# Four low weight parts of the second attention ordered behind the third-last step of the down chain, and a fourth PSUM bank for the transposes of the output projection

## The chip, the core and the metric

The kernel runs on one NeuronCore of a Trainium2 chip. A core has five engines with a queue each: TensorE (PE; its weight loads are shown apart as PEld), VectorE (DVE), ScalarE (ACT), GpSimd (POOL) and SyncE (SP). Each works its queue in order, and they wait for one another by semaphores. Transfers between HBM and the on-chip SBUF are ordered by SP, POOL and ACT and run on 16 DMA engines. TensorE writes to PSUM, which has eight banks of 128 x 512 fp32 values.

The metric is the device time of one execution in microseconds (us), median of three runs; less is better.

## What is computed

One step of an encoder of two layers in fp32: 1024 prompt tokens (eight tiles of 128) and eight running streams of 16 tokens each (a ninth tile, the "sample" tile, called ST). Cut to what matters:

```
for layer in range(2):
    x = rmsnorm(h, g_attn[layer])
    if layer == 0:  q, k, v = split(x @ w_qkv_a)         # window of 128, ALiBi, sinks
    else:           k, v = split(rmsnorm(h, g_kv) @ w_kv); q = x @ w_q_b   # 8 chunks back, learned bias
    h = h + attend(rmsnorm(q), rmsnorm(k), v) @ w_o[layer]
    h = h + square(relu(rmsnorm(h, g_mlp[layer]) @ w_up[layer])) @ w_down[layer]
```

Model width 1024, 16 heads of 64, 4 key/value heads, 4096 hidden values. The outputs are both token sets after layer 1 and the new keys and values.

## The kernel before, in words

**Numbers in two parts.** Every operand x of a product is cut into a high part (a rounded copy) and a low part (x minus the high part). A product is then three matmuls: high x high, high x low, low x high. `split` (line 125) does it, the high part mostly on ACT (line 128), the low part on DVE (line 134). The attention's projection weights are also multiplied by the norm's gain: `split_g` (line 180) makes the high part of one 128 x 512 slice on POOL (line 185; on ACT in some loads of layer 0) and the low part on DVE (line 190).

**Stages.** Per layer (`run`, line 1318): `attention`, `wo_phase` (the rest of the output projection, norm, and transposes for the MLP), `mlp_up`, `mlp_down`. The two MLP products use a fast matrix multiplication scheme of 20 products a half: `mlp_up` forms seven sums of inputs and weights, writes its results as 20 "forms" to DRAM (`hd`), and `mlp_down` reads them back. The profile has layer 0's down stage up to about 1144 us, then layer 1's attention to about 1618, its output projection to about 1670, and its MLP.

**Order of the work.** A planner (line 1864) simulates the program and orders each engine's instructions by readiness and priority. Some orders are forced by hand: `behind(a, b)` (line 747) puts b after a on their engine, without a wait.

**The down chain** (`mlp_down`, line 965) is 40 products n, each of 36 matmuls into three banks of `ps_c`. For product n DVE makes the low part of the form (`a`, line 134), the low part of the weights (`w`, line 134) and, where the weights are a sum of two slices, that sum in advance (line 1060: `s<-r,r`, or `r<-r,r` in place for the last products). Partial results are added by DVE (line 1174), or copied by ACT (line 1162) and added in DRAM by an accumulating transfer that POOL orders (lines 1165, 1179; line 1092 for whole tiles). `chain` (line 1112) ties all these DVE steps into one fixed order, product by product: low part of form n+1, low part of weights n+1, the sum for n+2, the additions of n. At the end of layer 0 the list of steps reads: ..., low form 38, low weights 38, sum 39, low form 39, low weights 39. The third from its end is therefore the sum for the last product, which starts at 1124.63 us in the profile. The loads of the forms (line 1024) are chained on SP; each takes one of three buffers and goes out when the product three before has left it.

**The start of the second attention** (line 1651). It is emitted after the down stage, with a priority raised by 1000 up to line 1691, so that it is planned into the end of the down chain. `load_block` (line 141) loads the key/value weights in four pieces of two 128-row slices: SP orders the transfer into a "raw" buffer (line 146), POOL makes the high parts, DVE the low ones, eight of each. There are only two raw buffers (line 1322), used in turn; then the first two token tiles X(0), X(1) (line 1421, loads at 1422) take the same two buffers. A buffer is free when both low parts of its piece are made. N(t) transposes X(t) on PE (line 210), cuts it (`hh` on ACT, `hl` on DVE), and K1(t) (lines 217 to 219) multiplies it by the key/value weights.

**The output projection** (`wo_phase`, line 643). `M(t)` finishes tile t in a bank of pool `m` (four banks) and norms it; `S(i)` forms four sums of two tiles on POOL (lines 697 to 700) in single buffers; `T(i)` and the sample tile call `turn` (line 687) 30 times. A turn is four transposes on PE into one bank of pool `g` (three banks), a high part on ACT (`sx`, line 128) and a low part on DVE (`sx`, line 134), after which the bank is free. DVE also makes weight parts for `mlp_up` and norms (line 641) in this time, and the planner puts the first products of `mlp_up` (lines 743 to 745, `ps_x`, `ps_z`) between the turns. `mlp_up` itself uses all eight banks, as does the attention; in `wo_phase` one is unused, the bank in which the attention keeps its projections (`ps_mm`).

Of the kernel before, what the change touches and what calls it, by code (L numbers as in the profile page):

```python
# [94 lines left out]
class Build:  # L95
# [84 lines left out]
    def split_g(self, hi, lo, raw, g, k0, act):  # L180
        nc = self.nc
        for k in range(raw.shape[1]):
            s = self.gcol[:, g * KC + k0 + k : g * KC + k0 + k + 1]
            if "g" in self.engs and not act:
                nc.gpsimd.tensor_scalar(hi[:, k], raw[:, k], s, 1.0, ALU.mult, ALU.mult)
            else:
                z = nc.scalar.activation(hi[:, k], raw[:, k], AF.Copy, scale=s)
                if act:
                    self.behind(self.lp, z)
            nc.vector.scalar_tensor_tensor(  # L190
                lo[:, k], raw[:, k], s, hi[:, k].bitcast(F32), ALU.mult, ALU.subtract
            )

    def wslot(self, kc=KC, n=512):
        self.nw += 1
# [447 lines left out]
    def wo_phase(self, layer, sx, x8, wo):  # L643
        nc = self.nc
        with ExitStack() as st:
            self.psum_pools(st, f"wo{layer}", dict(m=(4, 1), g=(3, 1)), dict(m="m", n="g"))
            work = self.pool(st, f"wow{layer}")
            small = self.pool(st, f"wosm{layer}", 2)
            osp, xs = {}, {}
            lo, hi = slice(0, 512), slice(512, 1024)  # L650

            def O(t, z):
                if t in self.kept:
                    xs[t] = self.kept[t]
                    return
                if len(xs) % 5 < 2:
                    xs[t] = self.rawp.tile([P, D], F32, tag="raw", name="x")
                else:
                    xs[t] = work.tile([P, D], F32, tag="x", name="x", bufs=3)
                nc.sync.dma_start(xs[t], self.xd[t])  # L660
                if t in self.wo_done:
                    return
                with self.tc.high_priority(WO_PRIO) if len(osp) < 2 else nullcontext():
                    load_o(t, z)

            def load_o(t, z):
                o = work.tile([P, 4, P], F32, tag=f"o{z}", name="o")
                oh = work.tile([P, 4, P], F32R, tag=f"oh{z}", name="oh")
                ol = work.tile([P, 4, P], F32R, tag=f"ol{z}", name="ol")
                self.last = oh.bitcast(F32)  # L670
                self.load_halves(layer, 1, t, o, lambda: self.last, nc.vector)
                self.split(oh, ol, o)
                osp[t] = oh, ol

            def M(t):
                x = xs[t]
                for n in range(2) if t not in self.wo_done else ():
                    nn = slice(n * 512, n * 512 + 512)
                    ps = self.psum("m", [P, 512], "ps_wo")
                    self.wo_proj(ps, *osp[t], wo, nn)  # L680
                    nc.vector.tensor_tensor(x[:, nn], ps, x[:, nn], ALU.add)
                if t not in self.wo_done:
                    nc.scalar.dma_start(self.xd[t], x)
                if t not in self.kept:
                    self.norm(small, work.tile([P, D], mybir.dt.bfloat16, tag="junk", name="junk"), x)

            def turn(src, dst, c, d):
                ps = self.psum("n", [P, 4, P], "ps_n")
                for k in range(4):
                    nc.tensor.transpose(ps[:, k, :], src[:, k * P : (k + 1) * P], self.ident)  # L690
                self.split(dst[0][:, d, c], dst[1][:, d, c], ps)

            def S(i):
                x1, x2 = xs[i], xs[i + NT // 2]
                s = self.sums() if i else self.sums0
                tt = nc.gpsimd.tensor_tensor
                tt(s[0], x2[:, lo], x2[:, hi], ALU.add)
                tt(s[1], s[0], x1[:, lo], ALU.subtract)
                tt(s[2], x1[:, lo], x2[:, lo], ALU.subtract)
                tt(s[3], x1[:, hi], s[1], ALU.subtract)  # L700
                return [x1[:, lo], x1[:, hi], x2[:, hi], *s]

            def T(i, src):
                c = slice(i * P, i * P + P)
                for p in (0, 1, 2, 3, 4, 5, 6):
                    turn(src[p], sx[p], c, slice(0, 4))

            order = WO_ORDER[layer]
            ready, pend = set(), []
            z = 0  # L710
            for t in order[:2]:
                O(t, z % 2)
                z += t not in self.wo_done
            for n, t in enumerate(order):
                if n + 2 < NTILE:
                    O(order[n + 2], z % 2)
                    z += order[n + 2] not in self.wo_done
                M(t)
                ready.add(t)
                for f in pend:  # L720
                    f()
                pend = []
                if t == ST:
                    def sample():
                        for h in range(2):
                            turn(xs[ST][:, h * 512 : h * 512 + 512], x8, slice(0, P), slice(4 * h, 4 * h + 4))
                    pend.append(sample)
                elif (t + 4) % NT in ready:
                    i = t % 4
                    T(i, S(i))  # L730
            for f in pend:
                f()
# [232 lines left out]
    def mlp_down(self, layer, out):  # L965
# [3 lines left out]
        with ExitStack() as st:  # L969
# [137 lines left out]
            split_h(0)  # L1107
            split_w(0)
            add_w(1)
            self.dve = None  # L1110

            def chain(z):
                if self.dve is not None:
                    self.behind(self.dve, z)
                self.dve = z
                return z

            self.behind(self.marks[-1], low[0][1])
# [139 lines left out]
    def run(self):  # L1258
# [9 lines left out]
        with ExitStack() as top:  # L1268
# [46 lines left out]
            ]  # L1315
            self.kv_out[1][ST] = flat(nkb_s), flat(nvb_s)
            y = lambda t: y_pf[t * P : (t + 1) * P, :] if t < NT else y_sf
            for layer in range(2):
                with ExitStack() as st:
                    low = st.enter_context(ExitStack())  # L1320
                    pools = (f"raw{layer}", 2), (f"wa{layer}", 1)
                    got = {n: self.pool(low, n, b) for n, b in pools[:: 1 if layer else -1]}
                    self.rawp, self.wa = got[f"raw{layer}"], [got[f"wa{layer}"]]
                    self.nw = 0
                    keep = self.pool(low, f"keep{layer}")
                    self.gb = keep.tile([P, D], F32, tag="gb", name="gb")
                    self.sums = lambda: [
                        keep.tile([P, 512], F32, tag=f"s{n}", name="s") for n in range(4)
                    ]
                    self.sums0 = self.sums()  # L1330
                    self.kept = {}
                    with ExitStack() as more:
                        self.wa.append(self.pool(more, f"wb{layer}"))
                        wo = self.attention(layer)
                    sx, x8, rp = self.up_pools(st, layer)
                    raw0 = self.up_raw(layer, rp, 0)
                    self.wo_phase(layer, sx, x8, wo)
                    low.close()
                    self.mlp_up(layer, sx, x8, rp, raw0)
                self.mlp_down(layer, y if layer else lambda t: self.xd[t])  # L1340
# [24 lines left out]
    def attention(self, layer):  # L1365
# [18 lines left out]
        with ExitStack() as st:  # L1384
# [248 lines left out]
            if A:  # L1633
                X(0)
                self.load_block(wkv, wkv_src, kv0, gkv, [0])
                X(1)
                N(0)
                self.load_block(wkv, wkv_src, kv0, gkv, [2])
                X(ST)
                N(1, "pt")  # L1640
                self.load_block(wkv, wkv_src, kv0, gkv, [4, 6])
                N(ST, "p")
            else:
                if 0 in psp:
                    X(0)
                if 0 in psp:
                    for k0 in range(0, KC, 2):
                        self.load_split(wkv, 0, [k0, k0 + 1])
                        if k0 == 2:
                            X(1)  # L1650
                else:
                    self.load_block(wkv, wkv_src, kv0, gkv)
                    X(0)
                    X(1)
                X(ST)
                N(0)
                N(1, "pt")
                if not cfg["late"]:
                    N(ST, "p")
# [247 lines left out]
```

## Time and profile before

| | |
|---|---|
| median of 3 runs | 2359.38 us (2356.24 to 2361.45) |
| the profiled execution's own time | 2359.46 us |
| its span, first to last instruction | 2357.7 us |
| PE busy | 2276.8 us (97%) |
| PEld / DVE / ACT / POOL busy | 80% / 73% / 57% / 27% |
| granted TensorE clock, mean | 0.993 |
| layer 0 output projection, last part | about 427 to 448 us |
| layer 0 down chain's end | 1144.27 us |
| layer 1 output projection, last part | about 1640 to 1672 us |

Busy times of different engines overlap. The span leaves out 1.8 us of the execution's own time, at its ends. In the timeline, a row gives start, duration, engine, line, operation, the tiles written and read, a count, and in brackets the idle time before it with what ended it. In a table by stages, "busy (x)" is the busy time and number of instructions of an engine in that stretch, PEclk the granted clock as a share of full speed, then the DMA engines' share and their rate.

### The profile page before, as it was taken

How to read it: one execution, taken by the hardware profiler on the slowest of the kernel's cores; microseconds unless marked ns; L12 is line 12 of the kernel's file. 1: busy time of each engine (PE TensorE's matmuls, PEld its weight loads, DVE VectorE, ACT ScalarE, POOL GpSimd, SP SyncE). 2: the span in 40 equal slices, each digit the busy share in tenths (PEclk: the TensorE clock that was granted, in tenths of full speed). 3: DMA queues.
4: the chain of work that ended last, by engine and by line, in shares of the span. 5: the costliest groups of instructions: out<-in, count | busy, mean ns of one | idle time of the engine just before them, and what ended most of it. 6: DMA issues, size and time to landing. Idle time of an engine off the chain costs nothing.

```text
span 2357.7 us, 33388 instructions
## 1 busy us (share of the span) xinstructions
PE 2276.8 (97%) x11429; PEld 1897.0 (80%) x11429; DVE 1716.9 (73%) x3075; ACT 1333.3 (57%) x2684; POOL 637.1 (27%) x950
## 2 busy tenths in 40 slices
PE   8998999899999999999999999998899999999999
PEld 6787877788888888777777778887788888878887
DVE  6888786766656578799567876777666566678987
ACT  3777674555555555444367666665655555555443
POOL 4434332313222111002333434344132132210011
PEclk9999999999999999999999999999999999999999
DMA  7435545234434677757653656555244343977567
GB/s 261 131 100 180 162 144 204 79 122 159 143 110 148 218 228 180 260 153 205 191 155 111 197 151 181 167 171 177 71 162 133 114 161 108 283 205 194 183 163 198
DMA packets 226714, 392.69 MB, mean 167 GB/s; under 512 B 51592, under 2 KB 126288, under 8 KB 226448
## 3 DMA queue, kind: packets, MB, share of 16 engines
q1 hardware_dynamic: 188816, 283.58, 37.7%
q0 software_dynamic: 36432, 102.26, 15.9%
q10 hardware_dynamic: 1296, 4.72, 0.5%
q8 instruction: 90, 1.47, 0.3%
q14 instruction: 80, 0.66, 0.1%
HBM read 236.51 MB, written 156.85 MB: 167 GB/s over the span
## 4 chain that ended last, share of the span: by engine, by line
PE 77%; DVE 8%; DMA 7%; ACT 4%; issue 3%; POOL 1%; SPq 0%; ACTq 0%; DVEq 0%; POOLq 0%
PE ps_c L743 7%; PE ps_c L744 7%; PE ps_c L745 7%; PE ps_x L743 5%; PE ps_x L745 5%; PE ps_x L744 5%; PE ps_mm L217 4%; PE ps_mm L219 3%; PE ps_mm L218 3%; PE ps_y L745 2%; PE ps_y L744 2%; PE ps_y L743 2%; DMA a<-hd 2%; PE ps_tr L324 2%; PE ps_mm L176 1%
## 5 line engine op out<-in xcount | busy, mean ns | idle before, releaser
L743 PE MATMUL ps_c<-w,a 128*128 128x512 f32 x960 | 375.8, 391 | 6.3 <-ACT o L1162 3.4
L744 PE MATMUL ps_c<-w,a 128*128 128x512 f32 x960 | 375.2, 391 | 6.5 <-DVE w L134 6.5
L745 PE MATMUL ps_c<-w,a 128*128 128x512 f32 x960 | 374.8, 390 | 0.0
L908 POOL DMA_DIRECT2D hd<-h x272 | 148.8, 550 | 595.8 <-ACT h L817 378.5
L743 PEld LDWEIGHTS ps_c<-w,a 128*128 128x128 f32 x960 | 180.9, 188 | 47.4 <-ACT o L1162 5.3
L744 PEld LDWEIGHTS ps_c<-w,a 128*128 128x128 f32 x960 | 181.1, 189 | 45.7 <-DVE w L134 8.2
L745 PEld LDWEIGHTS ps_c<-w,a 128*128 128x128 f32 x960 | 180.9, 188 | 37.7
L128 ACT CAST a<-a 128x1536 fp32r<-128x1536 f32 x80 | 118.6, 1483 | 144.4 <-DMA a<-hd 144.4
L217 PE MATMUL ps_mm<-w,hh 128*128 128x512 f32 x432 | 172.9, 401 | 7.7 <-DMA hh<-hTd 2.7
L134 DVE TENSOR_TENSOR a<-a 128x1536 fp32r<-128x1536 f32 x80 | 140.6, 1758 | 45.3 <-ACT a L128 45.3
L219 PE MATMUL ps_mm<-w,hl 128*128 128x512 f32 x432 | 171.7, 398 | 1.7 <-DVE hl L134 1.6
L218 PE MATMUL ps_mm<-w,hh 128*128 128x512 f32 x432 | 170.8, 395 | 0.2
L743 PE MATMUL ps_x<-sx,w 128*128 128x512 f32 (+1 forms) x408 | 157.8, 387 | 3.6 <-ACT h L864 2.5
L128 ACT CAST w<-s 128x2048 fp32r<-128x2048 f32 x56 | 107.1, 1912 | 95.8 <-DVE s L1060 84.8
L128 ACT CAST w<-ru 128x512 fp32r<-128x512 f32 (+1 forms) x160 | 110.0, 708 | 84.7 <-PE ps_y L744 32.0
L745 PE MATMUL ps_x<-sx,w 128*128 128x512 f32 (+1 forms) x408 | 154.1, 378 | 0.0
L744 PE MATMUL ps_x<-sx,w 128*128 128x512 f32 (+1 forms) x408 | 154.1, 378 | 0.0
L134 DVE TENSOR_TENSOR w<-s,w 128x2048 fp32r<-128x2048 f32 x56 | 128.2, 2289 | 35.0 <-ACT w L128 34.8
L1179 POOL DMA_DIRECT2D xp<-o x28 | 36.3, 1296 | 415.5 <-ACT o L1162 392.7
L134 DVE TENSOR_TENSOR w<-ru,w 128x512 fp32r<-128x512 f32 (+1 forms) x160 | 128.8, 807 | 15.1 <-ACT w L128 15.0
L134 DVE TENSOR_TENSOR ptl<-ps_tr,pth 128x512 fp32r<-128x512 f32 x180 | 122.5, 685 | 22.0 <-ACT pth L128 18.5
L816 ACT ACTIVATE h<-h 128x512 f32<-128x512 f32 (+1 forms) x102 | 61.9, 607 | 122.4 <-DVE h L866 93.3
(274 smaller groups left out, 6145.2 us busy)
## 6 DMA issues: line engine op xcount, KB each, us to landing
a<-hd SPq DMA_DIRECT2D x80, 768.0 KB, 5.6
hd<-h POOLq DMA_DIRECT2D x272, 192.0 KB, 2.5
ru<-in_w_up SPq DMA_DIRECT2D x64, 512.0 KB, 4.0
r<-in_w_down SPq DMA_DIRECT2D x32, 1024.0 KB, 9.7
xp<-o POOLq DMA_DIRECT2D x28, 768.0 KB, 9.2
o<-oTd SPq DMA_DIRECT2D x50, 256.0 KB, 3.8
x<-xp SPq DMA_DIRECT2D x23, 512.0 KB, 5.7
xp<-xo SPq DMA_DIRECT2D x18, 512.0 KB, 2.9
```

The source lines that it names most:

```text
L128: a = nc.scalar.copy(hi, src)
L134: return a, e.tensor_tensor(lo, src, hi.bitcast(F32), ALU.subtract)
L217: nc.tensor.matmul(ps, a, w[:, 0, k, :], start=(k == 0), stop=False)
L218: nc.tensor.matmul(ps, a, w[:, 1, k, :], start=False, stop=False)
L219: self.lp = nc.tensor.matmul(ps, b, w[:, 0, k, :], start=False, stop=(k == KC - 1))
L324: self.lp = nc.tensor.transpose(pt[:, i, :], get(i), self.ident)
L743: a = mm(ps, ah, bh, start=first, stop=False, skip_group_check=True)
L744: mm(ps, ah, bl, start=False, stop=False, skip_group_check=True)
L745: return a, mm(ps, al, bh, start=False, stop=last, skip_group_check=True)
L816: a = nc.scalar.activation(t, src, AF.Relu)
L908: return lambda p, z: self.nc.gpsimd.dma_start(self.hd[c // 4][:, p, c % 4], z)
L1179: nc.gpsimd.dma_start(dst, z, accum_op=ALU.add)
```

## The change

`chain` also keeps its steps in a list. In the second attention the first four low parts of the key/value weights (slices 0 to 3, the first two pieces) are each put behind the third step from the list's end. The other four are as they were. And pool `g` of `wo_phase` gets a fourth bank, in both layers, so that all eight are used.

```diff
@@ split_g
-            nc.vector.scalar_tensor_tensor(
+            z = nc.vector.scalar_tensor_tensor(
                 lo[:, k], raw[:, k], s, hi[:, k].bitcast(F32), ALU.mult, ALU.subtract
             )
+            if self.low_after:
+                self.behind(self.chained[-self.low_after.pop(0)], z)
@@ wo_phase
-            self.psum_pools(st, f"wo{layer}", dict(m=(4, 1), g=(3, 1)), dict(m="m", n="g"))
+            self.psum_pools(st, f"wo{layer}", dict(m=(4, 1), g=(4, 1)), dict(m="m", n="g"))
@@ mlp_down
-            self.dve = None
+            self.dve, self.chained = None, []
 
             def chain(z):
                 if self.dve is not None:
                     self.behind(self.dve, z)
                 self.dve = z
+                self.chained.append(z)
                 return z
@@ run
+            self.low_after = []
             for layer in range(2):
@@ attention, layer 1
                 else:
+                    self.low_after = [3, 3, 3, 3]
                     self.load_block(wkv, wkv_src, kv0, gkv)
```

## The prediction

> **What bounds the kernel now.** I read the busy time by stages first. Its columns are the stretch, its length, then per engine the busy time and count, the granted clock, the DMA engines' share and their rate.
>
> ```profile
> 427.00:448.00 21.00, 13.98 (x79) 11.16 (x78) 19.82 (x26) 12.79 (x23) 6.78 (x5) 0.76 0.24 76
> 448.00:760.00 312.00, 311.46 (x1610) 266.70 (x1609) 188.61 (x303) 172.19 (x331) 69.22 (x129) 1.00 0.38 127
> 1095.00:1148.00 53.00, 47.92 (x210) 38.71 (x208) 36.09 (x31) 18.49 (x20) 17.93 (x20) 0.97 0.70 178
> 1640.00:1672.00 32.00, 20.89 (x132) 16.64 (x131) 28.49 (x42) 20.07 (x37) 13.41 (x11) 0.89 0.22 70
> ```
>
> In the up stage (448 to 760) PE is busy 311.46 of 312.00 us: it sets the time, and what is saved ahead of it stays saved. The change touches the three other rows: the ends of the two output projections (PE idle 7.0 and 11.1 us) and the passage from the down chain to the second attention (5.1 us). In the projections' ends DVE is nearly full, 19.82 of 21.00 and 28.49 of 32.00 us.
>
> Next, who waited for whom on PE between 1088 and 1148, and the granted clock in the stretch behind the longer wait:
>
> ```profile
> PE ps_c L744 <- DVE w L134: 2.2, 1, 2.2
> PE ps_c L743 <- DVE x L1174: 1.6, 1, 1.6
> ```
>
> ```profile
> 1118.20:1123.00 4.80, 4.76 (x14) 3.78 (x15) 4.43 (x3) 2.42 (x2) 0.00 (x0) 0.64 1.05 281
> ```
>
> PE waits twice for DVE, and after the second wait the clock is 0.64 for 4.80 us, which costs 4.80 x 0.36 = 1.7 us more. The loss in the chain's end is 1.6 + 2.2 + 1.7 = **5.5 us**. DVE's own order in this time shows why:
>
> ```profile
> 1098.35 2.13 DVE L134 TENSOR_TENSOR a<-a 128x1536 fp32r<-128x1536 f32 x1
> 1100.39 3.37 DVE L190 SCALAR_TENSOR_TENSOR w<-raw,gcol,w 128x512 fp32r<-128x512 f32 x3
> 1103.69 2.28 DVE L134 TENSOR_TENSOR w<-r,w 128x2048 fp32r<-128x2048 f32 x1
> 1105.89 0.74 DVE L190 SCALAR_TENSOR_TENSOR w<-raw,gcol,w 128x512 fp32r<-128x512 f32 x1
> 1106.55 1.27 DVE L1174 TENSOR_TENSOR x<-x,ps_c 128x512 f32<-128x512 f32 x2
> 1107.75 2.28 DVE L1060 TENSOR_TENSOR r<-r,r 128x2048 f32<-128x2048 f32 x1
> ...
> 1115.90 2.28 DVE L134 TENSOR_TENSOR w<-r,w 128x2048 fp32r<-128x2048 f32 x1
> 1118.11 2.28 DVE L1060 TENSOR_TENSOR r<-r,r 128x2048 f32<-128x2048 f32 x1
> 1120.31 1.74 DVE L134 TENSOR_TENSOR a<-a 128x1536 fp32r<-128x1536 f32 x1
> 1122.42 2.29 DVE L134 TENSOR_TENSOR w<-r,w 128x2048 fp32r<-128x2048 f32 x1 [0.37 <-ACT w L128]
> 1124.63 2.28 DVE L1060 TENSOR_TENSOR r<-r,r 128x2048 f32<-128x2048 f32 x1
> 1128.62 1.76 DVE L134 TENSOR_TENSOR a<-a 128x1536 fp32r<-128x1536 f32 x1 [1.71 <-ACT a L128]
> 1133.47 2.29 DVE L134 TENSOR_TENSOR w<-r,w 128x2048 fp32r<-128x2048 f32 x1 [1.94 <-ACT w L128]
> 1147.39 1.29 DVE L134 TENSOR_TENSOR hl<-ps_n,hh 128x512 fp32r<-128x512 f32 x2 [11.62 <-ACT hh L128]
> ```
>
> ```profile
> 1098.00:1118.00 20.00, 7.44 (x8) 1.00 0.75 220
> ```
>
> The last row is L190 alone: the eight low parts of the second attention's weights take 7.44 of DVE's 20.00 us in the middle of the chain. Four stand ahead of the additions (1106.55) for which PE waits 1.6, all eight ahead of the weights (1115.90) for which it waits 2.2. Behind the chain's sums DVE has 1.71, 1.94 and 11.62 us free.
>
> **Part one, the order.** The third step from the list's end is the sum of 1124.63. Four low parts move behind it. The other four follow unasked, because there are two raw buffers; SP's queue shows it:
>
> ```profile
> 1102.69 0.37 SPq L146 DMA_DIRECT2D raw<-in_w_kv  x1
> ...
> 1106.66 0.37 SPq L146 DMA_DIRECT2D raw<-in_w_kv  x1
> ...
> 1113.65 2.68 SPq L1422 DMA_DIRECT2D x<-xp  x2
> ```
>
> The third piece is ordered at 1102.69, when two of the three low parts of 1100.39 are done; the fourth at 1106.66, when the part of 1105.89 is done; the token tiles from 1113.65. All of these now wait for the sum of 1124.63: all 7.44 us leave the chain, and two weight loads and two token loads move later on SP, past the last form loads. POOL's high parts of pieces three and four move past its accumulating transfers. What then sets the chain's end is worked from PE's spacing and the landing times between 1088 and 1130:
>
> ```profile
> 1105.16 0.39 PE L744 MATMUL ps_c<-w,a 128*128 128x512 f32 x1
> 1105.39 0.39 PE L745 MATMUL ps_c<-w,a 128*128 128x512 f32 x1
> ...
> 1144.27 1.94 PE L210 MATMUL ps_n<-identr,x 128*128 128x128 f32 x16
> ```
>
> ```profile
> a<-hd SPq DMA_DIRECT2D x4, 768.0 KB, 8.6
> raw<-in_w_kv SPq DMA_DIRECT2D x4, 512.0 KB, 5.6
> ```
>
> A product is 36 matmuls 0.23 us apart, 8.2 us. Without waits products 36 to 39 start at 1105.6, 1113.8, 1122.0 and 1130.2 and the chain ends at 1138.4 to 1138.8 (1144.27 - 5.5). DVE must be ahead of that. The last addition follows PE at 1105.6 and ends by 1106.3. Then low form 37 (1.7) and low weights 37 (2.2) are done at 1110.2, needed at 1113.8. Sum 38 (2.2), low form 38, low weights 38: its form load goes out when product 35 ends, 1105.6, and takes 8.6 by the median above; with about 1.5 us on ACT it is ready by 1115.7, so low weights 38 is done by 1119.6, needed at 1122.0. Sum 39 ends at 1121.8, and form 39 (ordered at 1113.8) is ready by 1123.9. The four low parts (0.74 each where POOL is quiet, 1.1 in the row of 1100.39) take 3.0 to 4.5 us, to 1126.3 at worst; last form and weights 3.9 more, 1130.2, needed at 1130.2. Behind the moved parts stand low form 39 and low weights 39, and PE's last product waits for these; the cover just holds at worst and has 1.5 us to spare at 0.74. So I take **-5.5 us** here; ends: 0 (if the new wait eats it, first rival) and -5.5.
>
> What is late next are the token tiles: from the sum's end 1.5 (two low parts), 5.6 (raw load), 1.4 (two high parts on POOL), 0.7, 5.6 (token load): 14.8 for X(0) if it lands like a weight load of its size, 1136.6; X(1) two low parts later, 1138.1. PE is free at 1138.8. The loads move into a time in which the DMA engines are less busy. I charge nothing, with 0.7 us to spare.
>
> [...]
>
> **Part two, the bank.** PE's waits in the two projections' ends, 427 to 448 and then 1640 to 1672, and one row of DVE:
>
> ```profile
> PE ps_n L690 <- DVE sx L134: 4.8, 4, 1.5
> ```
>
> ```profile
> PE ps_n L690 <- DVE sx L134: 8.6, 8, 2.0
> ```
>
> ```profile
> 1653.50 0.69 DVE L134 TENSOR_TENSOR sx<-ps_n,sx 128x512 fp32r<-128x512 f32 x1 [1.53 <-ACT sx L128]
> ```
>
> PE waits 13.4 us for a bank to be emptied. But the emptying is DVE's work, and none is removed: DVE has 1.2 us free in the first stretch and 3.5 in the second, so -4.7 is the most. The sure piece is the row of 1653.50, where DVE itself was short of a turn that one more bank would have held ready: 1.5; of the smaller gaps I take 0.5. **-2.0 us**, nearest to that row. The other end is not zero alone: turns that the planner now puts ahead of a product on PE could hold it, and one more wait of the size of those above (4.8 in 4) makes +1.2. The new bank's earlier user, the last `ps_mm`, is added by DVE before the fourth turn in layer 1; in layer 0 it is close and may hold one turn, inside that +1.2.
>
> Sum against the profiled execution: 2359.46 - 5.5 - 2.0 = **2352.0** us. Its own time lies 0.08 us from the median of 2359.38, so nothing is corrected. About 0.2% (4.7 us) is what a measurement here can tell from no change.
>
> **Rivals.**
>
> *POOL's queue holds the token tiles (slower).* The high parts of pieces three and four now share POOL with the accumulating transfers of the last products, which wait for PE.
>
> ```profile
> 1106.49 1.38 POOL L185 TENSOR_SCALAR w<-raw,gcol 128x512 fp32r<-128x512 f32 x2 [3.26 <-DMA raw<-in_w_kv]
> ...
> 1145.52 0.85 POOL L1165 DMA_DIRECT2D xp<-x  x1 [1.97 <-ACT x L1162]
> ```
>
> The last accumulate would stand at 1140.0 (1145.52 - 5.5), the first of that product two banks earlier, 1134.5. If the planner puts all four high parts behind the first: 1134.5 + 0.85 + 2.8 + 0.7 + 5.6 = 1144.5 for X(1), and part one's gain is just gone: 2357.5. Behind the last it is 1150.0, 5.7 later than the 1144.27 of before, with the clock's 1.7 behind the long wait 7.4: 2359.46 + 7.4 - 2.0 = **2364.9**. So it decides from the first accumulate on. For it: POOL keeps its order whatever lands. Against it: the attention's parts have the raised priority. 0.15 for the slow end, 0.18 for the middle, which late loads (landing of some 10 us instead of 5.6) would also give.
>
> *The bank brings nothing.* DVE's 19.82 of 21.00 speaks for it, the 1.53 us against it: 2359.46 - 5.5 = **2354.0**. [...] 0.18.
>
> *The order does nothing*: the planner would have to have placed the low parts late already; the rows of 1100.39 to 1115.90 exclude it.
>
> *The whole plan shifts.* The planner orders the second attention anew from a changed start, and nothing prices that from here: 0.07, mostly slower.
>
> **Chances and range.** Both parts as summed 0.42 (2349.3, with all of DVE's free time, to 2354.0), the bank for nothing 0.18, the middle 0.18, the slow end 0.15, another plan 0.07 (0.01 faster, 0.02 same, 0.04 slower). Faster 0.61, same 0.20, slower 0.19. The range reaches from 2347.5 (1.8 below the bound, for a plan that falls well) to the slow end, 2365.0.
>
> **What would show it.** In the changed profile: no L190 between the chain's steps before the last sum, four directly behind it; no PE wait for `x` L1174 or `w` L134 in products 36 and 37 and a clock of 1.00 there; the chain's end 5 to 6 us earlier against the start of the stage; X loads ordered after the last form load and landed before PE is free. In the projections, fewer waits of `ps_n` for `sx`, DVE without the gap of 1.53, and stretches shorter by 0.5 and 1.5 us. I am wrong if PE waits for the transposes of the second attention, if the last product waits for its weights behind the four low parts, or if the attention's stretch changes length by more than the chain's end does.

## The result and the profile after

The changed kernel takes **2352.90 us** (median of 9 runs, 2349.97 to 2356.76); the kernel before, run beside it, 2361.66 us (median of 9 runs, 2356.24 to 2365.26). The ratio is **0.9966, with a 95% interval of 0.9955 to 0.9976**: 5.7 to 10.6 us less. The profiled execution has a span of 2349.6 us (2357.7 before) and the same mean clock, 0.993.

The same stages as before, with the same columns:

```profile
427.00:448.00 21.00, 14.09 (x88) 12.13 (x87) 18.21 (x25) 11.96 (x24) 6.16 (x4) 0.84 0.23 76
448.00:760.00 312.00, 312.00 (x1602) 266.75 (x1601) 191.42 (x307) 171.93 (x330) 72.19 (x134) 1.00 0.39 129
1095.00:1148.00 53.00, 46.90 (x206) 38.47 (x205) 34.62 (x33) 17.56 (x20) 23.61 (x23) 0.94 0.79 192
1640.00:1672.00 32.00, 23.45 (x162) 20.71 (x161) 25.54 (x36) 18.82 (x38) 12.38 (x10) 0.89 0.15 50
```

The stretches are the same times from the span's start; the changed kernel reaches its down stage 3.8 us earlier, so the lower rows hold somewhat later work than before. The up stage is as full as it was. In the passage to the second attention (third row) PE is busy **less** than before, 46.90 us against 47.92, and at a lower clock (0.94 against 0.97), although this is where the order was changed. In layer 1's projection (fourth row) DVE is less busy than before, 25.54 against 28.49 us: part of its work has moved out of this stretch, to an earlier time. PE's waits from 1088 to 1150, and the stretch that had the clock of 0.64:

```profile
PE ps_mm L219 <- ACT hh L128: 5.4, 1, 5.4
PE ps_n L212 <- ACT x L1165: 0.7, 1, 0.7
```

```profile
1118.20:1123.00 4.80, 4.80 (x23) 3.98 (x22) 3.26 (x2) 1.96 (x2) 4.59 (x4) 1.00 1.00 265
1140.80:1145.00 4.20, 4.14 (x10) 3.26 (x11) 3.85 (x6) 1.48 (x3) 0.00 (x0) 0.50 0.71 190
```

Both waits in the chain are gone and its clock is 1.00. But there is a new wait of 5.4 us at the attention's first product, with a clock of 0.50 behind it. DVE's and then SP's timeline, in the form that the prediction showed:

```profile
1112.55 2.29 DVE L1062 TENSOR_TENSOR r<-r,r 128x2048 f32<-128x2048 f32 x1
1114.75 2.73 DVE L190 SCALAR_TENSOR_TENSOR w<-raw,gcol,w 128x512 fp32r<-128x512 f32 x4
1117.41 1.76 DVE L134 TENSOR_TENSOR a<-a 128x1536 fp32r<-128x1536 f32 x1
1120.19 2.29 DVE L134 TENSOR_TENSOR w<-r,w 128x2048 fp32r<-128x2048 f32 x1 [1.02 <-ACT w L128]
1123.00 4.04 DVE L190 SCALAR_TENSOR_TENSOR w<-raw,gcol,w 128x512 fp32r<-128x512 f32 x4 [0.52 <-POOL w L185]
```

```profile
1116.19 1.69 SPq L146 DMA_DIRECT2D raw<-in_w_kv  x2
1125.31 2.10 SPq L1426 DMA_DIRECT2D x<-xp  x2
```

Four low parts stand directly behind the last sum (1112.55), the other four behind the last weights, and the token tiles X(0), X(1) are ordered only at 1125.31. That is as drawn in the prediction. What followed is seen on ACT, which the prediction did not read, then on POOL and PE:

```profile
1129.18 1.06 ACT L203 ACTIVATE junk<-x 128x1024 bf16<-128x1024 f32 x1 [9.02 <-DMA x<-xp]
...
1130.24 0.57 ACT L1165 ACTIVATE x<-ps_c 128x512 f32<-128x512 f32 x1
1132.16 1.06 ACT L203 ACTIVATE junk<-x 128x1024 bf16<-128x1024 f32 x1 [1.35 <-DMA x<-xp]
...
1133.22 1.06 ACT L1165 ACTIVATE x<-ps_c 128x512 f32<-128x512 f32 x2
1140.13 1.07 ACT L128 CAST hh<-ps_n 128x512 fp32r<-128x512 f32 x2 [5.84 <-DMA xp<-x]
1141.42 1.07 ACT L128 CAST hh<-ps_n 128x512 fp32r<-128x512 f32 x2 [0.22 <-DMA xp<-x]
```

```profile
1134.16 1.77 POOL L1168 DMA_DIRECT2D xp<-x  x2
```

```profile
1132.63 1.03 PE L212 MATMUL ps_n<-identr,x 128*128 128x128 f32 x8
1134.34 1.09 PE L212 MATMUL ps_n<-identr,x 128*128 128x128 f32 x8 [0.67 <-ACT x L1165]
1140.86 0.76 PE L219 MATMUL ps_mm<-w,hh 128*128 128x512 f32 x1 [5.43 <-ACT hh L128]
```

Read it as one queue feeding the next. ACT's queue has the squares of the token tiles (L203, for the norm's statistics) **ahead of** its copies (L1165) of the last product's three banks. The squares wait 9.02 us for X(0) and 1.35 for X(1), so the second and third copies start only at 1133.22, when PE has left the chain (1132.63). On POOL the transfers that add these copies in DRAM are ordered at 1134.16. `hh` waits for them by its rows (`<-DMA xp<-x`), 5.84 us, and PE for `hh`. Before, the same squares ran early, because X was there early, and the copies followed PE bank by bank:

```profile
1130.02 1.05 ACT L201 ACTIVATE junk<-x 128x1024 bf16<-128x1024 f32 x1
...
1141.74 0.60 ACT L1162 ACTIVATE x<-ps_c 128x512 f32<-128x512 f32 x1 [2.12 <-PE ps_c L745]
1144.46 0.60 ACT L1162 ACTIVATE x<-ps_c 128x512 f32<-128x512 f32 x1 [2.12 <-PE ps_c L745]
1146.77 1.08 ACT L128 CAST hh<-ps_n 128x512 fp32r<-128x512 f32 x2 [1.71 <-DMA xp<-x]
```

There the middle copy ran 2.5 us before PE left the chain (1141.74 against 1144.27), now 0.6 us behind it (1133.22 against 1132.63).

PE's waits for a transpose bank, in layer 0 from 427 to 448 and then in layer 1 from 1640 to 1672:

```profile
PE ps_n L692 <- DVE sx L134: 4.6, 3, 3.2
```

```profile
PE ps_n L692 <- DVE sx L134: 5.4, 3, 2.8
```

Layer 0 hardly changes (4.8 before), layer 1 goes from 8.6 to 5.4. What that does to DVE is seen best in the whole of layer 1's turns, from the first low part `sx` to the end of the last; first before, then after:

```profile
1621.55:1670.20 48.65, 37.80 (x214) 30.46 (x212) 40.43 (x60) 27.75 (x49) 24.79 (x20) 0.93 0.41 138
1630.00:1640.00 10.00, 10.00 (x52) 8.40 (x51) 8.06 (x13) 5.36 (x11) 5.11 (x5) 1.00 0.66 237
```

```profile
1619.01:1663.43 44.42, 36.76 (x213) 30.83 (x212) 40.96 (x59) 26.85 (x49) 25.41 (x20) 0.92 0.43 151
1630.00:1640.00 10.00, 10.00 (x60) 8.63 (x59) 10.00 (x19) 6.71 (x14) 3.46 (x5) 1.00 0.61 228
```

DVE's work is the same (40.43 and 40.96 us); its idle time fell from 8.22 to 3.46 us, and the stretch from 48.65 to 44.42. The second rows show a piece that the prediction's window, 1640 to 1672, had cut off: DVE was idle 1.94 us in 1630 to 1640, and is now full there. It stands in this row of the kernel before:

```profile
1636.87 1.29 DVE L681 TENSOR_TENSOR x<-ps_wo,x 128x512 f32<-128x512 f32 x2 [1.94 <-POOL s L700]
```

The row names one of POOL's sums, not a transpose, as what ended this gap. POOL's sums of that pair wait for transposes that still read their buffers, 2.10 us before and 1.20 us after, and start 6.2 us behind the layer's first `ps_wo` before (1626.88 and 1620.65), 5.4 us behind it after (1623.45 and 1618.10). That fits a bank that was missing some steps earlier, but no run shows this step by itself.

So the two traces together give a theory: **the order brought nothing and the bank brought everything**. The rival is what the prediction said: some 5.5 us by the order, 2.0 by the bank.

### The profile page after: what moved, and what is told of

Read it like the earlier page. It is cut to its first block, busy times and chain, and to the rows that moved or that the text cites. A ratio compares the mean times of both kernels' runs of the same rounds, so it can differ in the third digit from the quotient of the medians.

```text
span 2349.6 us, 33397 instructions
## 1 busy us (share of the span) xinstructions
PE 2273.2 (97%) x11429; PEld 1899.3 (81%) x11429; DVE 1718.3 (73%) x3075; ACT 1332.0 (57%) x2684; POOL 644.7 (27%) x950
## 4 chain that ended last, share of the span: by engine, by line
PE 73%; DVE 11%; DMA 8%; ACT 3%; issue 2%; POOL 2%; SPq 1%; ACTq 0%; DVEq 0%; POOLq 0%
PE ps_c L745 7%; PE ps_c L746 7%; PE ps_c L747 7%; PE ps_x L745 5%; PE ps_x L747 5%; PE ps_x L746 5%; PE ps_mm L219 3%; PE ps_mm L221 3%; PE ps_mm L220 3%; PE ps_y L747 2%; PE ps_y L746 2%; PE ps_y L745 2%; PE ps_tr L326 2%; DMA a<-hd 2%; DVE w L134 1%
## 5 line engine op out<-in xcount | busy, mean ns | idle before, releaser
L746 PEld LDWEIGHTS ps_c<-w,a 128*128 128x128 f32 x960 | 180.2, 188 | 42.7 <-DVE w L134 5.6
L134 DVE TENSOR_TENSOR ptl<-ps_tr,pth 128x512 fp32r<-128x512 f32 x180 | 122.5, 685 | 21.2 <-ACT pth L128 17.5
```

Of the source, the lines that this page charges most:

```text
L134: return a, e.tensor_tensor(lo, src, hi.bitcast(F32), ALU.subtract)
L746: mm(ps, ah, bl, start=False, stop=False, skip_group_check=True)
```

## The experiments

**The two parts alone.** The order without the bank, and the bank without the order:

```diff
 e1_order, from the changed kernel:
-            self.psum_pools(st, f"wo{layer}", dict(m=(4, 1), g=(4, 1)), dict(m="m", n="g"))
+            self.psum_pools(st, f"wo{layer}", dict(m=(4, 1), g=(3, 1)), dict(m="m", n="g"))
 e2_bank, from the kernel before:
-            self.psum_pools(st, f"wo{layer}", dict(m=(4, 1), g=(3, 1)), dict(m="m", n="g"))
+            self.psum_pools(st, f"wo{layer}", dict(m=(4, 1), g=(4, 1)), dict(m="m", n="g"))
```

> The order alone, three banks as before. Theory A (the prediction's terms): the chain's end is 5.5 us earlier and nothing is given back, so about 5.5 us below the kernel before. Theory B (read from the changed kernel's trace): the chain's end comes 5.9 us earlier, but the second attention's first product then waits about 5.4 us for its high part hh instead of 1.3, and the clock drops behind that wait, so only 0 to 2 us remain. In its trace: no wait of PE in products 36 to 39 by both; a wait for hh of over 4 us by B.

> The fourth bank alone, in both output projections. Theory A: about 2 us below the kernel before, 4.7 us at most. Theory B: most of the whole change's 8 us, 5 to 8 us below, about half in each projection, with PE's chain end in layer 0 still waiting 1.6 and 2.2 us.

Measured, beside the kernel before at 2363.97 us: the order alone 2364.05 us, ratio **1.0000** (0.9986 to 1.0013); the bank alone 2354.29 us, ratio **0.9968** (0.9953 to 0.9983), by the ratio 7.6 us less (4.0 to 11.1). PE's waits from 1088 to 1150, first with the order alone, then with the bank alone:

```profile
PE ps_mm L219 <- ACT hh L128: 5.7, 1, 5.7
```

```profile
PE ps_c L744 <- DVE w L134: 2.3, 1, 2.3
PE ps_c L743 <- DVE x L1174: 1.6, 1, 1.6
PE ps_mm L217 <- ACT hh L128: 1.6, 1, 1.6
```

The order takes away 2.3 + 1.6 and makes the wait for `hh` 4.1 us longer. The theory holds for the totals; the rival's 5.5 us lies outside the order's interval (its lower end is 3.3 us less). For the bank alone, its 2.0 us lies outside too (the nearer end is 4.0).

**Why the order brought nothing.** If the squares in ACT's queue are the cause, putting them behind the last copy must give the gain back. This mend was run with four banks, twice, and with three:

```diff
 e3_stats and e11_stats, from the changed kernel:
-        nc.scalar.activation(junk, x, AF.Square, accum_out=ssq)
+        z = nc.scalar.activation(junk, x, AF.Square, accum_out=ssq)
+        if self.stat_after:
+            self.behind(self.copies[-self.stat_after.pop(0)], z)
...
-                            nc.scalar.activation(adds[o][i], banks[i], AF.Copy, scale=float(v))
+                            self.copies.append(nc.scalar.activation(adds[o][i], banks[i], AF.Copy, scale=float(v)))
...
                     self.low_after = [3, 3, 3, 3]
+                    self.stat_after = [1, 1]
 e5_mend3: the same with g=(3, 1)
```

> Both parts, and the squares of the first two token tiles (statistics on ACT) put behind ACT's last copy of the down chain. Theory B: the copies of the last product stood behind these squares, which waited for late token tiles; so the accumulating transfers, and the high part hh that takes their memory, were late. Then the wait for hh falls from 5.4 to about 1.5 us and the time by 3 to 5 us below the whole change. Rival C: hh waits for the accumulating transfers' own landing, whatever ACT's order; then the wait stays over 4 us and the time is that of the whole change within 1 us.

> The order as in the change, the squares of the two token tiles put behind ScalarE's last copy of the down chain, and three banks as before the change. If ScalarE's queue ate part one's gain (squares that wait 9.0 us for late token tiles stand ahead of the copies, the copies ahead of the accumulating transfers, those ahead of hh), PE's wait for hh falls from 5.7 us (order alone) to about 2.2, the clock stays up behind it, and the time is 3 to 5 us below the kernel before (ratio about 0.9983). If the order is worth nothing for another reason (the attention stage absorbs an earlier start wherever it comes from), the time stays within 1.2 us of the kernel before, as with the order alone.

> The changed kernel with the squares behind ScalarE's last copy once more, on the chip of these runs. If the mended order (2.9 to 4.4 us below the kernel before with three banks) and the bank (7.6) add, 10 to 12 us below the kernel before and 3 to 5 below the changed kernel; if it gains no more than the kernels with earlier low parts, 7 to 9 us below the kernel before.

Measured: with three banks 2358.75 us, ratio **0.9980** (0.9968 to 0.9993), where the order without the mend had 1.0000. With four banks 2351.85 us, ratio 0.9953 (0.9935 to 0.9971), and on another chip 2350.17 us, ratio 0.9951 (0.9933 to 0.9969). ACT in the first of them, and PE's waits there and with three banks:

```profile
1136.49 0.60 ACT L1167 ACTIVATE x<-ps_c 128x512 f32<-128x512 f32 x1 [2.12 <-PE ps_c L749]
1139.21 0.60 ACT L1167 ACTIVATE x<-ps_c 128x512 f32<-128x512 f32 x1 [2.12 <-PE ps_c L749]
1139.71 1.05 ACT L203 ACTIVATE junk<-x 128x1024 bf16<-128x1024 f32 x1
```

```profile
PE ps_mm L221 <- ACT hh L128: 2.2, 1, 2.2
```

```profile
PE ps_mm L221 <- ACT hh L128: 1.9, 1, 1.9
```

The copies again follow PE bank by bank, and the wait for `hh` falls from 5.4 to 2.2 us, which also rules out that the transfers' own landing held it, whatever ACT's order (it would then have stayed above 4). With three banks the two intervals, with and without the mend, still overlap a little; the stages below separate them better. The cause is shown: in the changed kernel the moved loads were late for ACT's queue, not for PE. The margin for PE was thin, though. In the last run of the mend, `e12_mend_bank1` below, PE waits for the token tile X(1) itself:

```profile
PE ps_n L214 <- DMA x<-xp: 1.5, 1, 1.5
```

**The low parts one product earlier.** If late tokens are the trouble, an earlier place might keep both gains:

```diff
 e6_early, from the changed kernel (e7_both: the same from e3_stats):
-                    self.low_after = [3, 3, 3, 3]
+                    self.low_after = [6, 6, 6, 6]
 e8_after: the changed kernel again
```

> The changed kernel with the four low parts behind the sum of product 38 instead of 39, one product earlier; the other four again come behind the next ones. Weights and token tiles are then ordered some 7 us earlier, the squares no longer wait long, and the copies follow PE. Theory of the queue: PE's wait for hh falls from 5.4 to below 2.5 us, the chain loses at most 1 us (four low parts of 0.7 us against about 1.5 us of slack before low weights 38), and the time is 2 to 5 us below the changed kernel. Rival: DVE has no room there, PE waits again for the weights of products 38 or 39 (2 to 4 us with the lower clock), and the time is that of the changed kernel or up to 2 us above.

> The last kernel with the squares also behind ScalarE's last copy. If the late token tiles are the whole cause, this adds nothing to the low parts behind sum 38 (within 1 us of it), since squares that don't wait don't hold the copies. If the copies are held by something else on ScalarE as well, it is 1 to 3 us below it.

> The changed kernel again, beside the three others on one chip, as the mark for them: 7 to 11 us below the kernel before (0.9953 to 0.9972 of it), with PE's wait for hh of 5 to 6 us and one wait of 0.7 for the copy x.

Measured, beside the kernel before at 2361.72: earlier low parts 2354.18 us, ratio 0.9969 (0.9956 to 0.9982); with the squares behind the copies as well 2354.10 us, 0.9964 (0.9950 to 0.9978); the changed kernel 2356.77 us, 0.9975 (0.9962 to 0.9988), a little less gain than was expected of it. The intervals overlap; times alone don't separate them. The waits of the first and second say more:

```profile
PE ps_c L746 <- DVE w L134: 2.7, 1, 2.7
PE ps_mm L219 <- ACT hh L128: 2.0, 1, 2.0
```

```profile
PE ps_c L748 <- DVE w L134: 2.5, 1, 2.5
PE ps_mm L221 <- ACT hh L128: 1.6, 1, 1.6
```

Both theories were half right. The wait for `hh` falls, as one said; PE waits again for the weights of the last product, as the rival said. And my reason was wrong: the squares still waited long for X(0), as ACT shows with the earlier low parts alone:

```profile
1132.10 1.06 ACT L203 ACTIVATE junk<-x 128x1024 bf16<-128x1024 f32 x1 [8.70 <-DMA x<-xp]
```

The weights did go out earlier, 312.0 us behind the down stage's first product instead of 318.0 (1111.33 - 799.36 and 1116.19 - 798.18), but their first high part on POOL starts only 10.5 us after the order (1121.83) instead of 4.0 (1120.16), and the token loads went out at the same point as in the changed kernel: 327.2 and 327.1 us behind that product. The copies were held less only because the chain itself was late.

**The bank by layers, and a fifth.**

```diff
 e4_bank0:  g=(3 if layer else 4, 1), from the kernel before
 e9_bank1:  g=(4 if layer else 3, 1), from the kernel before
 e12_mend_bank1:  g=(4 if layer else 3, 1), from e3_stats
 e10_bank5, from e2_bank:
-            self.psum_pools(st, f"wo{layer}", dict(m=(4, 1), g=(4, 1)), dict(m="m", n="g"))
+            self.psum_pools(st, f"wo{layer}", dict(m=(3, 1), g=(5, 1)), dict(m="m", n="g"))
```

> The fourth bank in layer 0's output projection only. Theory A: 0.5 us below the kernel before. Theory B: 3 to 4 us below, the rest of the bank's gain being layer 1's.

> The kernel before with the fourth bank in the second layer's output projection alone. In the profiles of before and of the bank alone, the time from the layer's first three sx low parts to its last is 48.7 and 43.4 us, so DVE's idle time of 5.1 us there has gone. If the parts add, this gives 4 to 6 us below the kernel before (the bank in both layers 7.6, in the first alone 1.3 to 2.7), and DVE's waits of 1.94 and 1.53 us are gone. If the bound of the prediction held (1.5 to 3.5 us for this layer), the time is at most 3.5 us below, and the rest of the 7.6 came from elsewhere.

> The changed kernel with the squares behind the copies, and the fourth bank in the second layer's output projection alone. Before it stand 0.9981 of the kernel before with three banks and 0.9951 to 0.9953 with four in both layers. By the stages of the profiles taken so far, layer 1 is 4 to 5 us shorter by its bank and layer 0 about 1 us: then this stands at 0.9955 to 0.9963, and its time from the first product of layer 1's output projection to the first of its down chain is 396 to 400 us (402 to 405 with three banks). If the run with the bank in layer 1 alone (0.9997) is to be believed, it stands at 0.998 like three banks, and the gain needs both.

> The bank alone, with five banks for the transposes and three for the products in both layers instead of four and four. PE still waits 5.4 and 5.2 us for banks with four. If DVE's idle time was what the fourth bank filled, little is left (DVE is busy 9.9 of each 10 us from 1630 to 1660), so the fifth gives at most 1 us, or loses 1 to 3 where products now wait for one of three banks. If every wait of PE for a bank costs time, the fifth takes another 3 to 5 us off, at 0.9950 of the kernel before or lower.

Measured: layer 0 alone 2362.63 us, ratio 0.9989 (0.9976 to 1.0002), which decides between neither of its two theories. Layer 1 alone 2360.25 us, ratio 0.9997 (0.9982 to 1.0011), which missed what was expected. Layer 1 with the mended order 2352.68 us, ratio **0.9949** (0.9930 to 0.9968), as good as both layers with it. So the reading that the gain needs both layers falls. Five banks: 2364.03 us, ratio 1.0001 (0.9988 to 1.0014), so the gain is gone; both expectations had it smaller or larger, not lost.

Runs of one kernel scatter by some 10 us here (6.8 to 17.5 us from a kernel's fastest to its slowest run), and the traces say where: the first matmul of layer 0's output projection, ahead of which nothing was changed, starts at 380.9 to 386.9 us in the 14 profiles. So stages are compared instead, each as the time between the starts of two matmuls in one profile: D from the first to the last `ps_c` of layer 0, K from the first `ps_c` of layer 0 to the second attention's first `ps_mm`, L from the first `ps_c` of layer 0 to layer 1's first `ps_wo`, W from that `ps_wo` to layer 1's first `ps_c`. (For before these matmuls start at 802.00, 1144.04, 1147.50, 1620.65 and 2023.12.) Bold marks D where the order is as in the change, K and L where it is also mended, and W where layer 1 has four banks.

| kernel | D | K | L | W |
|---|---|---|---|---|
| before | 342.0 | 345.5 | 818.7 | 402.5 |
| bank in layer 0 | 341.1 | 344.5 | 818.1 | 404.1 |
| bank in layer 1 | 343.4 | 347.1 | 822.1 | **397.8** |
| bank alone | 340.6 | 344.4 | 820.9 | **397.5** |
| five banks | 342.7 | 345.9 | 819.9 | 405.3 |
| order alone | **334.8** | 342.9 | 820.1 | 405.4 |
| after | **334.2** | 342.7 | 819.9 | **399.2** |
| after, again | **335.1** | 344.2 | 817.9 | **401.7** |
| mended, three banks | **335.7** | **339.8** | **817.7** | 402.3 |
| mended, four | **334.7** | **339.0** | **816.0** | **401.5** |
| mended, four, again | **334.2** | **338.4** | **814.7** | **396.4** |
| mended, four in layer 1 | **335.0** | **339.8** | **814.8** | **400.4** |
| earlier | 338.6 | 342.8 | 819.2 | **400.0** |
| earlier, mended | 339.5 | 343.3 | 818.6 | **397.4** |

By means of the groups: without the order D is 342.0, K 345.5 and L 819.9 (five profiles). With it D is 334.7, 7.2 us shorter; K 343.3, only 2.2 shorter; L 819.3, 0.6 shorter (three profiles). So 5.0 of 7.2 us go back at the attention's start, and 1.6 within the attention, where the lowered clock behind the wait for `hh` alone costs an estimated 2.1 us (4.20 us at 0.50 in the changed kernel). Mended, K is 6.2 us and L 4.2 us shorter (four profiles). W is 403.5 us with three banks in layer 1 (four profiles) and 399.1 with four (nine): the bank of layer 1 is worth **4.4 us**, also in the profile of layer 1 alone, whose runs did not show it (that profile is of the fastest of its twelve runs, 2352.75 us). In layer 0, from the first `ps_wo` to the start of the last low part `sx`, it is 63.6 us with three banks (five profiles) and 62.9 with four (eight): 0.7 us.

A fifth bank gave nothing on the turns (in layer 1, from the first `sx` to the start of the last, 43.5 us, with four 42.7), while the up stage paid. PE's waits from 1640 to 1690, and the up stage's beginning, with five and then with four banks:

```profile
PE ps_n L690 <- DVE sx L134: 5.6, 3, 1.9
PE ps_x L743 <- ACT h L869: 3.4, 1, 3.4
PE ps_n L690 <- POOL s L698: 1.6, 1, 1.6
```

```profile
1672.00:1700.00 28.00, 25.85 (x180) 25.01 (x181) 11.28 (x19) 14.15 (x34) 2.76 (x5) 0.88 0.22 66
```

```profile
1672.00:1700.00 28.00, 28.00 (x192) 26.01 (x191) 14.08 (x22) 15.93 (x37) 2.76 (x5) 1.00 0.23 74
```

PE still waits 5.6 us for banks, and that is no reserve: DVE is idle 6.4 us in these turns, but its gaps end on loads and steps of the norm, none on a transpose. The first product of the up stage starts 26.6 us behind layer 1's first `ps_wo` (1649.56 and 1623.00) instead of 22.5 (1643.94 and 1621.46), and PE then waits 3.4 us for what ACT makes of it. Two sizes changed at once here (five banks for turns, three for products), so which of them moved that product was not told apart.

**A version better than both.** The mended kernel with four banks stands at 0.9953 and 0.9951 of the kernel before, with four in layer 1 only at 0.9949; the changed kernel at 0.9966 and 0.9975. All three lie below both, though neighbouring intervals overlap.

## Why the prediction was right, and where it was wrong

The time was forecast at 2352.0 and came out at 2352.9 us. The **sum was right by luck: both its terms were wrong**, in opposite directions: the order 0 instead of -5.5 (the end that the prediction named but did not choose), the bank -7.6 by its runs (4.0 to 11.1 less), or -5.1 by the stages, instead of -2.0.

- *The chain.* Right. No L190 stands between its steps, four stand behind the last sum, the clock is 1.00, the waits of 1.6 and 2.2 us are gone, and the last product does not wait for its weights. Forecast 5.5 us, measured 7.2. The last ten products show 6.2 of it: they take 81.6 us in the kernels with this order and 87.3 to 88.8 without. The other 1.0 lies ahead of the moved parts and is not explained.
- *The token tiles.* The landing times were right, though not term by term. They were put at 1136.6 and 1138.1 with the chain's end at 1138.8; the chain ended at 1132.63, so that is 1130.4 and 1131.9, and the squares that waited for them start at 1129.18 and 1132.16. For X(0) each of the two transfers took about 4.0 us (1116.19 to 1120.16 and 1125.31 to 1129.18) where 5.6 was put, and the work of POOL and DVE between them 5.1 us where 2.1 was put. The step that failed is the next: "I charge nothing, with 0.7 us to spare". It asked only whether PE has the tiles in time. The first reader of a tile is ACT, in whose queue its squares stand ahead of the last copies. The list of instructions behind the waiting one was made for DVE and POOL, not for ACT.
- *What PE then lost.* The new wait is 3.8 us longer than the 1.6 us that the bank alone shows at that place, and the clock behind it is 0.50 for 4.20 us, by estimate 2.1 us more. The wait of 0.7 us for the copy stands beside it. Up to the first `ps_mm`, where K ends, that makes 4.5 us, against 5.0 by the means of D and K; the clock's 2.1 us come behind it. That PE waits at the second attention's transposes was one of the prediction's own signs of being wrong.
- *The bank.* The mechanism was right in the main: with one more bank DVE has less idle time and the same work. That every gap was DVE short of a turn is argued; the row of 1653.50 shows it, that of 1636.87 names POOL. The size failed, at "nearest to that row": one gap of 1.53 us was taken as the sure piece, and the smaller ones for 0.5. The bound of 4.7 us was nearer to the truth, and had itself been read from a stretch beginning at 1640, 3 us behind a gap of 1.94. DVE's idle time over all of layer 1's turns fell by 4.76 us.
- *Rivals.* POOL's queue did not hold the tokens: its high parts ran from 1120.16, ahead of the last product's transfers, which were ordered from 1131.14 on. The result of its middle case, part one's gain just gone, came true by another queue. "The bank brings nothing" is refuted by the bank alone. "The whole plan shifts" is refuted: the order leaves PE's list of instructions as it was, and the parts' effects add within their intervals.
- *The layers.* The prediction gave 0.5 us to layer 0 and 1.5 to layer 1. The stages have 0.7 and 4.4. The expectation for the bank alone, about half in each, missed too.

Open: of the 6.2 us that the mended order saves up to the attention's first product, 4.2 are left at layer 1's output projection. That stage lasts 473.2 to 476.5 us without the order and 475.0 to 477.9 with the mend, so the ranges overlap. Part of the 2 us is the clock: in two of the four mended profiles (`e3_stats`, `e5_mend3`) it is 0.64 over the 4.80 us behind the wait for `hh` (2.2 and 1.9 us long), an estimated 4.80 x 0.36 = 1.7 us. In a third (`e11_stats`, wait of 2.1 us) seven matmuls there take 0.63 us each, where 0.39 is their time at 1.00. In the fourth (`e12_mend_bank1`, wait of 1.0 us), where the clock is 1.00, the stage is the shortest of them; in the kernel before it is 1.00 there too, behind a wait of 1.3 us. The rest was not tried. Why the runs of the bank in layer 1 alone do not show what its profile shows is open too; scatter can do it, since the interval reaches to 4.2 us less.

## What to carry to other kernels

When a load is moved later, list **every** reader of it, and for each the instructions queued behind that reader on its engine; the first to suffer may be an engine that is half idle (ACT here, 57% busy), and the price shows two engines further on. When an engine is nearly full, look for its idle gaps over the whole stage, not from a round time on. With DVE's work unchanged, a spare buffer could give at most that idle time here (8.22 us, of which 4.76 went), and the largest gap that it closed named another engine; with a fifth bank none of DVE's gaps ended on a transpose, and nothing more was gained. And take a total that fits for what it is; only the parts run alone showed that it was made of two errors.

## What the runs showed of the hardware

The clock behind a wait did not follow the wait's length alone. With the earlier low parts, PE's wait of 2.7 us ends at 1130.13 and that of 2.0 us at 1142.14. The 4.80 us behind each:

```profile
1130.10:1134.90 4.80, 4.77 (x21) 3.96 (x22) 0.62 (x4) 2.67 (x5) 0.91 (x2) 1.00 0.50 177
1142.10:1146.90 4.80, 4.76 (x13) 3.58 (x14) 1.22 (x2) 0.65 (x2) 0.00 (x0) 0.64 1.05 297
```

Behind the longer wait the clock is 1.00, behind the shorter one 0.64. With the mend as well it is 0.64 behind the wait of 2.5 us and 1.00 behind that of 1.6:

```profile
1130.96:1135.76 4.80, 4.79 (x14) 3.79 (x15) 0.00 (x0) 0.60 (x1) 0.00 (x0) 0.64 0.52 181
1144.20:1149.00 4.80, 4.78 (x20) 3.75 (x21) 2.75 (x5) 1.44 (x3) 1.45 (x3) 1.00 0.97 304
```

The wait of 2.2 us behind which the prediction counted 1.7 us of clock is there with five banks too. There the first matmul behind it takes 0.50 us and the next ones 0.39 to 0.40, as ahead of it (0.39), while in the changed kernel, in the stretch with the clock at 0.50, they take 0.63. What decides beside the length, no run here shows.

So a wait of some 2 us here may cost about 1.7 us more (an estimate, 4.80 x 0.36), or nothing. And kernels whose instructions are the same up to layer 0's output projection reach it up to 6 us apart (380.9 to 386.9 us), which is nearly as much as this whole change is worth (8.0 us by the ratio): parts of it can be told apart only within a profile's stages or over many runs.
